# Spreading every norm's inverse root over the partitions: matrix products against transposes

## The chip, the cores and the metric

The kernel runs on one core of one Trainium2 chip. The metric is device time in microseconds (us) of one execution, taken as the median of several runs. Times inside an execution come from one profiled execution, and are counted from the start of its span.

## The reference

One layer of an encoder over 1024 tokens of width 1024, in float32: a norm, one combined projection, two kinds of attention side by side (group A: a sliding window with a sink; group B: a neighbourhood on a 16 x 64 grid), a norm for each group, one output projection, then a norm, a gated MLP with a convolution of width 3 along the tokens, and a last norm. Every norm is the same function:

```python
def rmsnorm(x, g):
    xf = x.astype(jnp.float32)
    y = xf * lax.rsqrt(jnp.mean(xf * xf, axis=-1, keepdims=True) + EPS)
    return (y * g.astype(jnp.float32)).astype(x.dtype)
...
hn = rmsnorm(h, norm_mix[l])
proj = jnp.einsum('bsd,de->bse', hn, w_in[l])
...
mix = jnp.concatenate([rmsnorm(o_a, norm_a[l]), rmsnorm(o_b, norm_b[l])], axis=-1)
h = h + jnp.einsum('bse,ed->bsd', mix, w_out[l])
hn = rmsnorm(h, norm_ffn[l])
h = h + conv_gated_mlp(hn, w_gate[l], w_up[l], conv_w[l], conv_b[l], w_down[l])
return rmsnorm(h, norm_final)
```

So five norms are computed: the first, those of group A and of group B, the middle one ahead of the MLP, and the last.

## The kernel before, in words

**Layout.** Activations are kept transposed: a tile has 128 features on its partitions and the 1024 tokens along its free axis, worked on in two halves h of 512 tokens. Large products split each float32 operand into a high and a low part of a reduced type and issue three products of 128x512 for each pair of blocks (lines 144 to 146 in `block`, 866 to 868 in `group`).

**The norms.** The sum over features runs across partitions, so TensorE does it. ACT squares the tiles and DVE adds them; then `inverse_narrow` multiplies each block of 128 tokens of the squares by a column of ones (L181), which leaves the sums in a narrow tile: token t of block c sits on partition t, column c. ACT takes the root (L184) and DVE the reciprocal (L185) of this 128 x 4 tile `v`. The features' tiles need the value of a token on all partitions, along the free axis. This is the work of `widen` (L192): for each of its n columns, a 128x128 block of the PSUM tile `wide` gets v's column along its free axis, the same on all partitions. The weights operand is v's column repeated 128 times (`to_broadcast`), the streamed operand is the identity `ident`, a slice of the tile `cst`.

**Who calls widen.** Four columns are one half of 512 tokens.
- First norm: both halves in one go; ACT copies them into `rstd1` (L626), with which DVE evacuates the first projections (`evacuate`, L199).
- Group A: `wide_a`, both halves between attention units; ACT copies them into `rstda` (L708), with which DVE scales `mixa` (L711).
- Group B: one half, then weights and some filling products, then the other half; DVE scales `mixb` straight from PSUM (L834), ACT makes the high part (L835), DVE the low part `mgl` (L836). Around it DVE also adds group A's output products to the residual (L553), and makes the low parts of output weights (L821).
- Middle norm: the first half between output products of the second half, the second half between the first products of the MLP; DVE scales the tiles in `normed` (L895).
- Last norm: `finish` calls widen twice, once for DVE (L1287) and once for a copy by ACT (L1281) that POOL uses for two of the eight feature tiles (L1285). It is called with four columns for the second half, and with two columns for each quarter of the first half; the last call stands at the end of the kernel, with the output's DMAs behind it (L1288).

**Transposes elsewhere.** The kernel already issues transposes of float32 tiles of 128x128 on TensorE: `split_v` turns the values (tile `vt`, L280, eight of them per call), and the attention units turn the probabilities (tile `pt`, L389 in group A and L462 in group B).

**What sets the order.** TensorE's order is the program's own: its queue is under a manual schedule, and group A's and B's attention, the projections and the output products are interleaved by hand (a generator `filler`, taken from at set rates). The order of DVE and ACT is chosen by a scheduler while the program is built, from estimated durations and priorities; a change in what an instruction is thought to cost can change that order. In the MLP's start, four units of weights come in at once (`pure`, `head_weights`): loads into three buffers `raw` (SP's queue), sums and differences of weights on DVE (L904, L912), and their high and low parts on ACT and DVE (L855, L856). `Gated` evacuates the products z and y with DVE (L1016, L1022, L1026).

PSUM tiles named by tag share two banks per tag; `widen` draws from the tag `pt` in every call, as the transposed probabilities do.

Of the kernel before, what the change touches and what calls it, by code (L numbers as in the profile page):

```python
# [53 lines left out]
def hybrid_layer(tc, xT, w_in, w_out, w_gate, w_up, w_down, small, sink, rpb, consts, rope, out):  # L54
    nc = tc.nc
    with ExitStack() as ctx:
# [19 lines left out]
        def bank(name, tag):  # L76
            return psum.tile([128, HALF], F32, name=name, tag=tag)
# [12 lines left out]
        ident = cst[:, K_ID:K_ID + 128]  # L90
# [85 lines left out]
        def inverse_narrow(sqs, dim, tag, n=4):  # L176

            ps = bank("ss", tag)
            for i, sq in enumerate(sqs):
                for c in range(n):  # L180
                    nc.tensor.matmul(ps[:, c:c + 1], sq[:, c * 128:(c + 1) * 128], ones[:, 0:1], start=c == 0 and i == 0,  # L181
                                     stop=i == len(sqs) - 1, skip_group_check=True)
            v = cpool.tile([128, 4], F32, name="v4", tag="v4", bufs=4)
            nc.scalar.activation(v[:, 0:n], ps[:, 0:n], AF.Sqrt, bias=eps, scale=float(D) / dim)  # L184
            nc.vector.reciprocal(v[:, 0:n], v[:, 0:n])  # L185
            return v

        def widen(v, tag, n=4):

            wide = bank("sw", tag)  # L190
            for c in range(n):
                nc.tensor.matmul(wide[:, c * 128:(c + 1) * 128], v[:, c:c + 1].to_broadcast([128, 128]), ident,  # L192
                                 start=c == 0, stop=True, skip_group_check=True)
            return wide


# [428 lines left out]
        for h in range(2):  # L625
            nc.scalar.activation(rstd1[:, tsl(h)], widen(vs1[h], "pt"), AF.Copy)  # L626
# [77 lines left out]
        def wide_a():  # L704
            live["op"] += 1
            norm["a"] = big("rstda", "op")
            for h in range(2):
                nc.scalar.activation(norm["a"][:, tsl(h)], widen(norm["v"][h], "pt"), AF.Copy)  # L708
# [120 lines left out]
        for h in range(2):  # L829
            wide = widen(vb2[h], "pt")  # L830
            for i in range(4):
                x = mix[4 + i][:, tsl(h)]
                hi, lo = (t[:, tsl(h)] for t in mg[4 + i])
                nc.vector.scalar_tensor_tensor(x, x, col(C_NB + i), wide, op0=ALU.mult, op1=ALU.mult)  # L834
                nc.scalar.activation(hi, x, AF.Copy)  # L835
                nc.vector.tensor_tensor(lo, x, f32(hi), op=ALU.subtract)  # L836
            if h == 0:
                wo = [load_wo(d, wpool) for d in range(2)]
                fill(3)
# [86 lines left out]
        for h in range(2):  # L926
            for d in range(KT):
# [6 lines left out]
                if h == 1 and d == 1:  # L934
                    v = inverse_narrow([total[0]], D, "pt")
# [5 lines left out]
                if h == 1 and d == 2:  # L941
                    wide = widen(v, "pt")
# [137 lines left out]
        v = inverse_narrow([total[1]], D, "pt")  # L1080
        units[1].p2()
        wide = widen(v, "pt")
# [375 lines left out]
```

## Time and profile before

| what | us |
|---|---|
| median of 3 runs | 1103.57 (1101.68 to 1103.87) |
| the profiled execution | 1103.74 |
| its span, first to last instruction | 1101.9 |
| DVE busy | 858.5 (78%) |
| ACT busy | 552.9 (50%) |

The profile lists each instruction with its start, length, engine, line and tiles (out<-in). "PE" is TensorE's products and "PEld" its weight loads, which overlap the products; "xN" counts instructions. In brackets stands how long the engine had been idle before an instruction and what released it. The list of waits sums these idle times by the waiting instruction. The length of a product includes time in which the next is already running, so that the distance from one start to the next is the measure of what a product costs in a stream. In the view by windows, each row gives a window, its length, and the busy time and number of instructions of TensorE, its loads, DVE, ACT and POOL, then the granted clock of TensorE (1.00 is full), the busy share of the DMA engines and GB/s.

### The profile page before, as it was taken

To read this page: it belongs to the slowest core of one execution; us is meant where nothing else is said; L and a number is where in the kernel's file an instruction comes from. 1 tells how busy PE (TensorE), PEld (TensorE's weight loads), DVE (VectorE), ACT (ScalarE), POOL (GpSimd) and SP (SyncE) were. 2 spreads that over 40 slices of the span, in tenths; PEclk is the share of its full clock that TensorE was granted. 3 is DMA by queue.
4 is the path that set the end of the run, shared out by engine and by line. 5 is a ranking of instruction groups with operands and counts; after the bars stand their busy time and mean duration, and the time that the engine had idled before them with its cause. 6 is when DMAs were issued, how large, how long until landed. Compare 5 with 4: busy or idle time off the path is not lost.

```text
span 1101.9 us, 15051 instructions
## 1 busy us (share of the span) xinstructions
PE 1079.2 (98%) x5190; PEld 901.0 (82%) x5190; DVE 858.5 (78%) x1565; ACT 552.9 (50%) x1042; POOL 109.2 (10%) x188
## 2 busy tenths in 40 slices
PE   8999999999999999999999999999999999999996
PEld 6888788888888888887788888888888778888886
DVE  7688787667688689899988877887787857886843
ACT  7457676556676544545434343433434643533631
POOL 2223333222232100000000000000000000000001
PEclk9999999999999999999999999999999999999998
DMA  7222122222225136214342232322233888774824
GB/s 271 72 72 68 48 58 68 77 76 77 77 67 159 68 127 240 96 39 162 124 161 89 104 124 77 132 98 106 96 112 109 277 288 289 258 227 165 270 79 154
DMA packets 68365, 144.95 MB, mean 132 GB/s; under 512 B 8128, under 2 KB 18880, under 8 KB 68288
## 3 DMA queue, kind: packets, MB, share of 16 engines
q1 hardware_dynamic: 57632, 118.16, 33.6%
q10 hardware_dynamic: 10656, 25.82, 6.2%
q8 instruction: 41, 0.67, 0.2%
q14 instruction: 36, 0.29, 0.1%
HBM read 103.58 MB, written 28.57 MB: 120 GB/s over the span
## 4 chain that ended last, share of the span: by engine, by line
PE 86%; DVE 7%; DMA 3%; ACT 2%; issue 2%; POOL 0%; SPq 0%; DVEq 0%; ACTq 0%; POOLq 0%
PE pj L144 7%; PE pj L145 7%; PE pj L146 7%; PE dn L866 6%; PE dn L867 6%; PE dn L868 6%; PE z L868 5%; PE z L866 5%; PE z L867 5%; PE x L866 3%; PE s L327 3%; PE x L867 3%; PE x L868 3%; PE y L868 3%; PE y L867 3%; PE y L866 3%
## 5 line engine op out<-in xcount | busy, mean ns | idle before, releaser
L866 PE MATMUL dn<-xd,whi 128*128 128x512 f32 (+1 forms) x330 | 124.9, 378 | 2.3 <-ACT c L1294 2.3
L868 PE MATMUL dn<-xd,wlo 128*128 128x512 f32 (+1 forms) x330 | 124.4, 377 | 0.0
L867 PE MATMUL dn<-xd,whi 128*128 128x512 f32 (+1 forms) x330 | 124.2, 377 | 0.0
L855 ACT ACTIVATE whi<-ws 128x512 fp32r<-128x512 f32 (+1 forms) x100 | 60.2, 624 | 122.3 <-DVE ws L972 80.4
L866 PE MATMUL z<-hg,whi 128*128 128x512 f32 x264 | 103.0, 390 | 1.0 <-DVE gs L1022 1.0
L144 PE MATMUL pj<-xgh,whi 128*128 128x512 f32 x248 | 104.0, 419 | 0.0
L868 PE MATMUL z<-hg,wlo 128*128 128x512 f32 x264 | 103.1, 390 | 0.6 <-DVE wlo L856 0.6
L867 PE MATMUL z<-hg,whi 128*128 128x512 f32 x264 | 102.7, 389 | 0.0
L353 ACT ACTIVATE p<-p,nm 128x385 f32<-128x385 f32 (+3 forms) x128 | 75.3, 588 | 51.7 <-DVE nm L349 50.6
L146 PE MATMUL pj<-xgh,wlo 128*128 128x512 f32 x248 | 97.6, 393 | 0.0
L145 PE MATMUL pj<-xgl,whi 128*128 128x512 f32 x248 | 97.2, 392 | 0.0
L357 POOL TENSOR_SCALAR p<-p,sm 128x384 f32<-128x384 f32 (+1 forms) x128 | 74.1, 591 | 215.9 <-DVE sm L355 201.5
L856 DVE TENSOR_TENSOR wlo<-raw,whi 128x512 fp32r<-128x512 f32 (+1 forms) x102 | 66.6, 673 | 22.7 <-ACT whi L855 22.4
L363 DVE TENSOR_TENSOR pl<-pt,ph 128x384 fp32r<-128x384 f32 (+2 forms) x108 | 63.0, 588 | 24.5 <-ACT ph L362 23.2
L855 ACT ACTIVATE whi<-raw 128x512 fp32r<-128x512 f32 (+1 forms) x102 | 60.5, 613 | 42.7 <-DMA raw<-in_w_down_dram 19.3
L856 DVE TENSOR_TENSOR wlo<-ws,whi 128x512 fp32r<-128x512 f32 (+1 forms) x100 | 66.8, 683 | 18.7 <-ACT whi L855 18.7
L1285 POOL TENSOR_TENSOR h<-h,wide 128x256 f32<-128x256 f32 (+1 forms) x6 | 5.4, 920 | 718.7 <-ACT wide L1281 718.7
L1177 ACT ACTIVATE xd<-xd 128x512 fp32r<-128x512 f32 x77 | 47.1, 627 | 55.0 <-DMA xd<-x 53.5
L866 PEld LDWEIGHTS dn<-xd,whi 128*128 128x128 f32 x330 | 62.5, 189 | 14.0 <-ACT c L1294 2.8
L868 PEld LDWEIGHTS dn<-xd,wlo 128*128 128x128 f32 x330 | 62.4, 189 | 11.5
L867 PEld LDWEIGHTS dn<-xd,whi 128*128 128x128 f32 x330 | 62.5, 190 | 11.1
L362 ACT ACTIVATE ph<-pt 128x384 fp32r<-128x384 f32 (+2 forms) x108 | 55.2, 515 | 32.0 <-PE pt L462 25.0
(211 smaller groups left out, 2686.0 us busy)
## 6 DMA issues: line engine op xcount, KB each, us to landing
xd<-x SPq DMA_DIRECT2D x77, 256.0 KB, 5.1
raw<-in_w_down_dram SPq DMA_DIRECT2D x72, 256.0 KB, 3.4
raw<-in_w_gate_dram SPq DMA_DIRECT2D x22, 512.0 KB, 3.6
raw<-in_w_up_dram SPq DMA_DIRECT2D x22, 512.0 KB, 3.8
x<-c ACTq DMA_DIRECT2D x22, 512.0 KB, 2.6
raw<-in_w_in_dram SPq DMA_DIRECT2D x32, 256.0 KB, 3.0
raw<-in_w_down_dram SPq DMA_DIRECT2D x36, 192.0 KB, 3.9
x<-t ACTq DMA_DIRECT2D x11, 512.0 KB, 2.6
```

Source lines behind the costliest of these rows:

```text
L144: nc.tensor.matmul(ps, w[0], x[0][:, tsl(h)], start=first, stop=False)
L145: nc.tensor.matmul(ps, w[0], x[1][:, tsl(h)], start=False, stop=False)
L146: nc.tensor.matmul(ps, w[1], x[0][:, tsl(h)], start=False, stop=last)
L353: nc.scalar.activation(p[:, j, 0:e], p[:, j, 0:e], AF.Exp, bias=nm, scale=-1.0, accum_out=sm[:, j:j + 1])
L357: nc.gpsimd.tensor_scalar(p[:, i, 0:m], p[:, i, 0:m], sm[:, i:i + 1], 1.0, op0=ALU.mult, op1=ALU.mult)
L362: nc.scalar.activation(ph[:, 0:n], ps[:, 0:n], AF.Copy)
L363: nc.vector.tensor_tensor(pl[:, 0:n], ps[:, 0:n], f32(ph[:, 0:n]), op=ALU.subtract)
L855: nc.scalar.activation(hi, src, AF.Copy)
L856: nc.vector.tensor_tensor(lo, src, f32(hi[:, :, :]), op=ALU.subtract)
L866: nc.tensor.matmul(ps, w[0], x[0], start=first and i == 0, stop=False, skip_group_check=True)
L867: nc.tensor.matmul(ps, w[0], x[1], start=False, stop=False, skip_group_check=True)
L868: nc.tensor.matmul(ps, w[1], x[0], start=False, stop=last and i == len(ws) - 1, skip_group_check=True)
```

## The change

In `widen`, the product of the repeated column and the identity is written as a transpose of the repeated column, with the same operands, into the same place. Flags of accumulation that the product carried go with it.

```diff
             wide = bank("sw", tag)
             for c in range(n):
-                nc.tensor.matmul(wide[:, c * 128:(c + 1) * 128], v[:, c:c + 1].to_broadcast([128, 128]), ident,
-                                 start=c == 0, stop=True, skip_group_check=True)
+                nc.tensor.transpose(wide[:, c * 128:(c + 1) * 128], v[:, c:c + 1].to_broadcast([128, 128]), ident)
             return wide
```

Nothing else is edited. In the built program, the order of instructions on TensorE, POOL and SP is as before. The scheduler gives DVE another order in four places (the evacuation L199 behind the first norm; L834, L836 and L553 around group B's norm; L885, L890, L904 and L856 around the first half of the middle norm; L904, L1016 and L1022 in the MLP's start) and ACT in two (L184 and L855 around the first half of the middle norm; L855, L873 and L1011 in the MLP's start). Everything in the steady part of the MLP and after it keeps its order.

## The prediction

> **What bounds the kernel now.** I read the page first, then the waits of TensorE, then the spread's own line beside that of an operation that already is a transpose, then the order of time around each place where the spread runs.
>
> ```profile
> span 1101.9 us, 15051 instructions
> ...
> PE 1079.2 (98%) x5190; PEld 901.0 (82%) x5190; DVE 858.5 (78%) x1565; ACT 552.9 (50%) x1042; POOL 109.2 (10%) x188
> ```
>
> TensorE works for 98% of the span, so what it is spared shortens the run unless a wait behind it takes the gain. These are the waits of TensorE, in us, number and longest:
>
> ```profile
> PE dn L866 <- ACT c L1294: 2.3, 1, 2.3
> ...
> PE sw L192 <- DVE v L185: 0.6, 1, 0.6
> ...
> PE sw L192 <- DVE pl L363: 0.3, 1, 0.3
> ```
>
> The largest is 2.3 us and there are few; the spread (sw) itself waits twice. So I treat TensorE's own stream as the bound nearly everywhere and look for the exceptions one by one.
>
> **The change: what one spread costs.** The line of the spread (L192), and the transposes of split_v (L280), whose operands have the same shape, type and places (data loaded as weights, identity streamed):
>
> ```profile
> L192 PEld LDWEIGHTS sw<-cst,v x96: 185/190/192, 39.4 to 1094.3; 128*128 128x128 f32 x96
> L192 PE MATMUL sw<-cst,v x96: 270/275/376, 39.6 to 1094.4; 128*128 128x128 f32 x96
> ```
>
> ```profile
> L280 PEld LDWEIGHTS vt<-cst,t x48: 138/141/146, 44.6 to 301.7; 128*128 128x128 f32 x48
> L280 PE MATMUL vt<-cst,t x48: 270/273/332, 44.8 to 301.8; 128*128 128x128 f32 x48
> ```
>
> widen is called 14 times: twice each for the first norm, group A, group B and the middle norm, and six times in the last one. Ten of the calls spread four columns, the last four spread two: 48 columns. The trace has 96 records, so a float32 matrix product leaves **two** records, each with its weight load. split_v runs 6 times with 8 transposes each, 48, and the trace has 48 records: a float32 transpose leaves **one**. The change therefore takes 48 pairs of load and product out of TensorE's stream.
>
> What a record is worth is read from start to start, not from its 275 ns, since they overlap. Eight records of the spread:
>
> ```profile
> 390.49 1.05 PE L192 MATMUL sw<-cst,v 128*128 128x128 f32 x8
> 391.29 0.48 PE L144 MATMUL pj<-mgh,whi 128*128 128x512 f32 x1
> ```
>
> that is 0.80 us. Sixteen of them, in the last norm:
>
> ```profile
> 1071.82 1.95 PE L192 MATMUL sw<-cst,v 128*128 128x128 f32 x16
> 1073.52 0.36 PE L866 MATMUL dn<-xd,whi 128*128 128x256 f32 x1
> ```
>
> 1.70 us. Eight transposes, and four:
>
> ```profile
> 44.81 1.03 PE L280 MATMUL vt<-cst,t 128*128 128x128 f32 x8
> 45.60 0.48 PE L144 MATMUL pj<-xgh,whi 128*128 128x512 f32 x1
> ```
>
> ```profile
> 151.65 0.60 PE L389 MATMUL pt<-cst,p 128*128 128x128 f32 x4
> 152.00 0.48 PE L144 MATMUL pj<-xgh,whi 128*128 128x512 f32 x1
> ```
>
> 0.79 and 0.35 us. Each further record costs (1.70 - 0.80) / 8 = 0.11 us, and a transpose costs no more; the change halves their number. A call of four columns saves 0.80 - 0.35 = **0.45 us**; two calls back to back save 1.70 - 0.79 = **0.91 us**. That the weights are one column repeated, and not a full tile, is new for a transpose but not for the load: the spread of before loads the same repeated column. This unknown lies between the transposes' own rows and a record of twice the length, which would eat the whole gain; I take the transposes' rows, as the nearest.
>
> **Place by place.** *First norm, pair:* 0.91. Behind it stand ACT's copy and then DVE:
>
> ```profile
> 41.30 0.69 DVE L199 TENSOR_TENSOR t<-pj,rstd 128x512 f32<-128x512 f32 x1 [3.20 <-ACT rstd L626]
> ```
>
> DVE idles 3.20 us for the spread's result, so the consumers start earlier with it and TensorE's later waits on them move along. In the changed program DVE takes both halves of one projection, then both of the other, instead of alternating; the first rotation can then start after two products instead of three. I count nothing for that.
>
> *Group A, two separate calls:*
>
> ```profile
> 289.97 1.06 PE L192 MATMUL sw<-cst,v 128*128 128x128 f32 x8
> 291.36 1.16 PE L192 MATMUL sw<-cst,v 128*128 128x128 f32 x8 [0.34 <-DVE pl L363]
> 292.28 0.47 PE L144 MATMUL pj<-xgh,whi 128*128 128x512 f32 x1
> ```
>
> ```profile
> 290.75 0.56 DVE L363 TENSOR_TENSOR pl<-pt,ph 128x384 fp32r<-128x384 f32 x1 [0.25 <-ACT ph L362]
> ```
>
> The second call waits for its PSUM bank, which DVE frees at 290.75 + 0.56 = 291.31 whatever the first call costs. So the first call's gain turns into 0.45 us more of that wait: **0**. The second saves 0.45, and what ACT and DVE do with its result moves with it.
>
> *Group B, two calls:* both inside a stream of products with no wait near: 2 x 0.45 = 0.90. Here the changed program orders DVE's L834, L836 and L553 otherwise: both L553 come sooner, and one operation that stood ahead of the second now stands behind it, ahead of the weights for the next products (L821).
>
> ```profile
> 402.06 0.69 DVE L553 TENSOR_TENSOR h<-pj,xr 128x512 f32<-128x512 f32 x1 [0.17 <-PE pj L146]
> ...
> 405.39 0.68 DVE L821 TENSOR_TENSOR wo<-raw,wo 128x512 fp32r<-128x512 f32 x1
> ```
>
> DVE waits for TensorE at that L553 already (0.17 us), so the weights come up to one operation, 0.68 us, later. No wait of TensorE for L821 is in its list, so there is room of unknown size: between 0 and 0.68 us I charge 0, and keep the other end for rival 1.
>
> *Middle norm, first half:* 0.45, same stream. *Second half:*
>
> ```profile
> 459.09 1.05 PE L192 MATMUL sw<-cst,v 128*128 128x128 f32 x8
> 459.90 0.48 PE L866 MATMUL x<-hg,whi 128*128 128x512 f32 x1
> ```
>
> ```profile
> 459.73 0.69 DVE L856 TENSOR_TENSOR wlo<-ws,whi 128x512 fp32r<-128x512 f32 x1 [2.29 <-ACT whi L855]
> 460.34 2.72 DVE L895 SCALAR_TENSOR_TENSOR h<-h,par,sw 128x512 f32<-128x512 f32 x4
> ...
> 492.86 0.69 DVE L1022 TENSOR_TENSOR gs<-z,c 128x512 f32<-128x512 f32 x1 [0.22 <-PE z L868]
> ```
>
> ```profile
> 460.00:513.00 53.00, 52.77 (x233) 43.06 (x232) 52.53 (x83) 26.28 (x42) 0.00 (x0) 1.00 0.17 56
> ```
>
> ```profile
> 512.83 0.50 PE L868 MATMUL z<-hg,wlo 128*128 128x512 f32 x1 [0.23 <-DVE wlo L856]
> ```
>
> From 460 to 513 DVE is busy 52.53 of 53 us (third busy figure of the window). It starts on L895 only after L856, not at the spread's end, so a faster spread does not start it sooner. TensorE comes 0.45 us earlier to a DVE that can give back only its small waits, such as the 0.22 us at 492.86, and TensorE's own wait at 512.83 grows by the rest. Between 0 and 0.45 I take 0.30.
>
> *Last norm:* the pair 0.91, then two calls of two columns back to back, eight records, 0.45. The last two calls stand in the tail, on the chain that ended last:
>
> ```profile
> 1093.58 0.70 PE sw L192 x4
> 1094.28 0.02 issue
> 1094.30 0.48 DVE h L1287
> ```
>
> DVE begins after the first call, four records. Two fewer save 2 x 0.11 = 0.22; the second call feeds ACT and POOL, which end before DVE does.
>
> **Sum:** 0.91 + 0.45 + 0.90 + 0.45 + 0.30 + 0.91 + 0.45 + 0.22 = 4.59 us. The profiled execution took 1103.74 us: 1103.74 - 4.6 = **1099.1 us**. It lay 0.17 us above the median of the three runs, less than the 2.2 us between their ends, so I leave it there.
>
> **The rivals.** (1) *A DVE-bound stretch takes more.* The gains ahead of the last norm, 3.0 us, all come before waits on DVE; only the last norm's 0.91 + 0.45 + 0.22 = 1.58 has none behind it. If half of the 3.0 us goes, 3.1 are left: 1100.7; if all goes, 1102.2. For it: the 52.53 of 53 us. Against: before 460, DVE idles for the spread or for TensorE. 0.24.
>
> (2) *The transposes do not overlap* and so the kernel gets slower. At 273 ns each, start to start, 48 take 13.1 us; 96 records at 1.70 / 16 take 10.2: 2.9 us more, 1106.6. It decides from 0.21 us per transpose. Against it stand 0.79 us for eight. A clock that fell would do the same; in the window that holds those eight it was full (the 1.00):
>
> ```profile
> 44.00:46.00 2.00, 2.00 (x15) 1.75 (x14) 1.38 (x4) 0.39 (x1) 0.00 (x0) 1.00 0.28 66
> ```
>
> [...] 0.04.
>
> (3) *Nothing is halved*: a transpose of a repeated column leaves two records. Then the time is that of before, 1103.7. 48 records for 48 calls of L280 speak against it. 0.03.
>
> (4) *DVE's new order costs.* Ahead of the L856 at 459.73 now stands the fourth difference of weights (L904), one place later than before, behind a load from DRAM. DVE's 2.29 us idle at 459.73 covers its 0.69 us and 1.6 us of lateness of that load; beyond, each us goes through the busy stretch to TensorE. Two us late past that cover would give 1101 to 1102; slower than before it makes the kernel only past 4.6. 0.07, of which 0.03 slower.
>
> **How the numbers follow.** The forecast, gains from 4.0 to 5.3, has 0.62. The low end is all 48 records (48 x 0.11 = 5.3, 1098.4) less half of the 2.2 us between the runs: 1097.2. The high end goes to 1101.6, most of rival 1; beyond lie its tail, and rivals 2, 3 and part of 4. A measurement of this kernel can tell about 0.2%, 2.2 us, from no change. Faster: 0.62 and three quarters of 0.24, 0.80; same: the rest of it, rival 3 and the milder part of 4, 0.13; slower: 0.07.
>
> **What would show it.** Right: 48 records of L192, 5142 on TensorE in all; spacing of eight (now four) from 0.80 to about 0.35, of the pairs from 1.70 to 0.79; the wait before group A's second call up from 0.34 to about 0.8; the wait at 512.83 up by up to 0.45. Wrong: two records per transpose, a spacing over 0.2 us, a granted clock under 1.00 at these places, or waits on DVE between 41 and 513 that grow by more than 1 us in all.

## The result, and the profile after

The kernel after takes 1096.26 us, median of 8 runs (1092.64 to 1098.07), where the kernel before took 1101.22 in 8 runs beside them (1100.26 to 1103.87): ratio 0.9938, 95% interval 0.9922 to 0.9954. The forecast was 1099.1, range 1097.2 to 1101.6: the sign is right, the gain larger than forecast, and the time lies below the range. Over the whole study, 78 runs of the kernel before have a mean of 1102.14 (standard error 0.20; 1098.42 to 1106.91) and 20 of the kernel after 1095.35 (0.43). The gain is **6.8 us, with a standard error of 0.5**, and 4.6 was forecast. ("Give or take" stands for a standard error everywhere below.)

The page of the kernel after; its profiled execution took 1097.33 us.

```profile
span 1095.5 us, 14955 instructions
...
PE 1073.6 (98%) x5142; PEld 895.3 (82%) x5142; DVE 857.4 (78%) x1565; ACT 550.6 (50%) x1042; POOL 109.0 (10%) x188
```

TensorE has 5142 records where it had 5190: 48 are gone, and the other engines' counts are as before. The spread's line (lines past 192 stand one lower now):

```profile
L192 PEld LDWEIGHTS sw<-cst,v x48: 132/136/137, 39.5 to 1089.3; 128*128 128x128 f32 x48
L192 PE MATMUL sw<-cst,v x48: 270/273/322, 39.8 to 1089.4; 128*128 128x128 f32 x48
```

One record per transpose, and its load is shorter too (136 against 190 ns). In the order of time, the middle norm's second half and the last norm's pair:

```profile
455.93 0.60 PE L192 MATMUL sw<-cst,v 128*128 128x128 f32 x4
456.28 0.48 PE L865 MATMUL x<-hg,whi 128*128 128x512 f32 x1
```

```profile
1068.71 1.03 PE L192 MATMUL sw<-cst,v 128*128 128x128 f32 x8
1069.50 0.36 PE L865 MATMUL dn<-xd,whi 128*128 128x256 f32 x1
```

Four transposes take 0.35 us from start to the next product, eight 0.79, as the prediction took from the other transposes. A repeated column costs here what a full tile costs, 0.79 us for eight.

Subtracting the starts of one and the same product in two traces gives the **shift** of TensorE's stream, and its step across a place is what that place gained. For the second half of the middle norm: the spread began at 459.09 and begins at 455.93, 3.16 earlier; the product behind it began at 459.90 and begins at 456.28, 3.62 earlier. The place gained 0.46. In this manner:

| place | forecast | measured |
|---|---|---|
| first norm, pair | 0.91 | 0.91 |
| group A, two calls | 0 + 0.45 | 0.60 |
| group B, two calls | 0.90 | 0.46 + 0.46 |
| middle norm, first half | 0.45 | 0.46 |
| middle norm, second half | 0.30 | 0.46 |
| last norm, pair and quarter | 0.91 + 0.45 | 0.92 + 0.46 |
| tail | 0.22 | 0.28 |
| sum | 4.59 | 5.01 |

So the places of the spread account for 5.0 us, and some **1.8 us** of the 6.8 were gained where no spread stands. Whether they come back, and from where they are, is what the experiments had to find.

The two places where the forecast had taken something off, group A's second call and TensorE's wait in the MLP's start, in the kernel after; between them ACT's copy of group A's first spread in the kernel before:

```profile
289.19 0.60 PE L192 MATMUL sw<-cst,v 128*128 128x128 f32 x4
289.84 0.59 ACT L707 ACTIVATE rstda<-sw 128x512 f32<-128x512 f32 x1
289.98 0.56 DVE L362 TENSOR_TENSOR pl<-pt,ph 128x384 fp32r<-128x384 f32 x1 [0.24 <-ACT ph L361]
290.49 0.65 PE L192 MATMUL sw<-cst,v 128*128 128x128 f32 x4 [0.69 <-ACT rstda L707]
```

```profile
291.06 0.60 ACT L708 ACTIVATE rstda<-sw 128x512 f32<-128x512 f32 x1 [0.34 <-PE sw L192]
```

```profile
509.21 0.50 PE L867 MATMUL z<-hg,wlo 128*128 128x512 f32 x1 [0.24 <-DVE wlo L855]
```

The wait before the second call did grow, from 0.34 to 0.69 us, but by 0.35 and not by the first call's 0.45. The profile now names ACT's copy of the first spread as what released it; that copy ends at 290.43. DVE's L362 ends only at 290.54, 0.05 us later than the call's start, so it is not what the call waited for. In the kernel before it was the other way: the call started 0.05 us behind DVE's end, and ACT's copy ended only at 291.66, 0.30 us behind that start. All three profiles of each kernel agree in this. At 509.21 the wait is 0.24 where it was 0.23: nothing was given back.

### The profile page after: what moved, and what is told of

It is laid out like the page before. It is cut to its first block, busy times and chain, and to the rows that moved or that the text cites. A ratio compares the mean times of both kernels' runs of the same rounds, so it can differ in the third digit from the quotient of the medians.

```text
span 1095.5 us, 14955 instructions
## 1 busy us (share of the span) xinstructions
PE 1073.6 (98%) x5142; PEld 895.3 (82%) x5142; DVE 857.4 (78%) x1565; ACT 550.6 (50%) x1042; POOL 109.0 (10%) x188
## 4 chain that ended last, share of the span: by engine, by line
PE 85%; DVE 9%; DMA 2%; ACT 2%; issue 1%; POOL 0%; SPq 0%; DVEq 0%; ACTq 0%; POOLq 0%
PE pj L144 7%; PE pj L145 7%; PE pj L146 7%; PE dn L865 6%; PE dn L867 6%; PE dn L866 6%; PE z L867 4%; PE z L865 4%; PE z L866 4%; PE s L326 3%; PE x L865 3%; PE x L866 3%; PE x L867 3%; PE y L867 3%; PE y L865 3%; PE y L866 3%
## 5 line engine op out<-in xcount | busy, mean ns | idle before, releaser
L855 DVE TENSOR_TENSOR wlo<-raw,whi 128x512 fp32r<-128x512 f32 (+1 forms) x102 | 66.5, 672 | 22.2 <-ACT whi L854 21.9
L362 DVE TENSOR_TENSOR pl<-pt,ph 128x384 fp32r<-128x384 f32 (+2 forms) x108 | 63.0, 588 | 24.5 <-ACT ph L361 23.3
L855 DVE TENSOR_TENSOR wlo<-ws,whi 128x512 fp32r<-128x512 f32 (+1 forms) x100 | 66.8, 683 | 18.4 <-ACT whi L854 17.3
```

Source lines behind the costliest of these rows:

```text
L362: nc.vector.tensor_tensor(pl[:, 0:n], ps[:, 0:n], f32(ph[:, 0:n]), op=ALU.subtract)
L855: nc.vector.tensor_tensor(lo, src, f32(hi[:, :, :]), op=ALU.subtract)
```

## The experiments

The kernels differ from before or after in `widen` alone or in one call of it. For kernels in which some calls are transposes and some products, `widen` has one more argument:

```diff
-        def widen(v, tag, n=4):
+        def widen(v, tag, n=4, turned=True):
             wide = bank("sw", tag)
             for c in range(n):
-                nc.tensor.transpose(wide[:, c * 128:(c + 1) * 128], v[:, c:c + 1].to_broadcast([128, 128]), ident)
+                if turned:
+                    nc.tensor.transpose(wide[:, c * 128:(c + 1) * 128], v[:, c:c + 1].to_broadcast([128, 128]), ident)
+                    continue
+                nc.tensor.matmul(wide[:, c * 128:(c + 1) * 128], v[:, c:c + 1].to_broadcast([128, 128]), ident,
+                                 start=c == 0, stop=True, skip_group_check=True)
```

Lines below stand three higher in them. "Ratio" is always to runs of the kernel before in the same series.

### Both kernels again

No edit.

> The kernel before, unchanged, once more. In the two profiled executions the changed kernel's span is 6.4 us shorter, of which 4.5 lie ahead of the last spread, 0.3 in it, and 1.6 behind the end of DVE's last products, where only the output's transfers land (1096.74 to 1101.9 before, 1091.97 to 1095.5 after). Theory A (the records alone count, the landing varies by itself from run to run): time within 0.2% of the kernel before, and the stretch from DVE's end to the end of the span may be anywhere from 3.5 to 5.2 us. Theory B (the change shortens the landing too): again 5.0 to 5.3 us there.

> The changed kernel, unchanged, once more. Theory A: 4.4 to 5.2 us faster than the kernel before in the median of many runs (0.40 to 0.47%), with a landing stretch anywhere from 3.5 to 5.2 us. Theory B: 6 to 7 us faster (0.55 to 0.65%), landing stretch 3.4 to 3.7 us each time.

> The changed kernel, unchanged, for more runs beside the next three. Over all runs so far it takes 6.6 us less than the kernel before (14 and 43 runs), while the shifts of TensorE's stream at the spreads and the tail's own 0.28 add up to 5.1. Theory A (records alone; what is over 5.1 is the scatter of the runs): 4.6 to 5.6 us faster than the kernel before (0.42 to 0.51%). Theory C (a product costs more than its two records, somewhere that the sites do not show): 6.0 to 7.0 us (0.55 to 0.63%).

Measured: the kernel before 1102.32 us (12 runs), ratio 1.0003 (0.9987 to 1.0018). The kernel after 1095.97, ratio 0.9937 (0.9917 to 0.9957), and 1094.8, ratio 0.9932 (0.9916 to 0.9949), 6 runs each. The gain repeats three times at 0.62 to 0.68%. All three profiles of after have the same steps at the spreads, to 0.01 us. The size of the gain is the one that theories B and C had, but B's reason does not hold: the stretch from DVE's end to the end of the span took 4.20 us in the repeated before, where B has 5.0 to 5.3. Theory C is put to the test by `twice` below.

### Part of the calls

`last_only` has transposes in `finish` alone (16 of 48 columns), `all_but_last` everywhere else (32).

```diff
-            wide, again = widen(v, "pt", n), widen(v, "pt", n)
+            wide, again = widen(v, "pt", n, True), widen(v, "pt", n, True)
```

(False in `all_but_last`; in `last_only` the default of `turned` is False.) The scheduler gives `last_only` the order of before on every engine, and `all_but_last` that of after.

> The kernel before with transposes only in the last norm (the calls from finish, 16 of the 48 columns); the order of all engines is that of the kernel before. Theory A: 0.93 + 0.46 + 0.28 = 1.7 us faster (0.15%), 5174 records on TensorE. Theory B: 3.3 us faster (0.30%), since the landing is shortened by the last spreads.

> The changed kernel with matrix products again in the last norm (32 of the 48 columns are transposes); DVE and ACT have the order of the changed kernel. Theory A: 3.0 to 3.3 us faster than the kernel before (0.28%): the shift of the stream by the last norm, 3.1 us in the changed kernel's trace. Theory B: the same 3.0 to 3.3 us. A rival for the earlier stages, that part of the shift there (0.4 us near 352 us) is one run's accident and not the change: 2.7 us. If it is above 4 us, the gain does not come record by record.

Measured: `last_only` 1100.05 us, ratio 0.998 (0.9968 to 0.9992); `all_but_last` 1096.74, ratio 0.9954 (0.9937 to 0.9971). Against the mean of all runs of before, their means (1100.09 and 1096.82) lie 2.1 and 5.3 us lower, which add up to more than the whole gain, within their scatter (0.5 and 0.7). In the trace `last_only` gains 0.92 + 0.46 at its two places inside the stream and nothing at the other spreads; with the tail's 0.22 to 0.28 that is 1.6 to 1.7. So it has about what its spreads are worth (theory A's 1.7, not B's 3.3). `all_but_last` gained more than both theories had, and more than the 4 us named beforehand as the sign that the gain does not come record by record alone: the surplus sits with the other 32 columns: their places sum to 5.01 - 1.66 = 3.35, and 5.3 was measured.

### More records of the same kind

`twice` issues each transpose twice into the same place, `four_times` four times.

```diff
-                nc.tensor.transpose(wide[:, c * 128:(c + 1) * 128], v[:, c:c + 1].to_broadcast([128, 128]), ident)
+                for _ in range(2):
+                    nc.tensor.transpose(wide[:, c * 128:(c + 1) * 128], v[:, c:c + 1].to_broadcast([128, 128]), ident)
```

> Every transpose is issued twice into the same place, so the spread leaves 96 records again, all transposes; DVE and ACT have nearly the order of the kernel before. Theory A: the time of the kernel before, within 0.1%. Theory C: still 1.0 to 1.9 us faster than the kernel before (0.09 to 0.17%). If transposes did not overlap, it would be slower than the kernel before by over 2 us.

> Every transpose is issued four times: 192 records, 144 more than in the changed kernel. Theory A: 144 x 0.11 = 15.8 us more than the changed kernel, less up to 0.7 that a wait in group A takes up, so 10 to 11 us slower than the kernel before (0.9 to 1.0%). A price of 0.14 us per record, as 6.6 us over 48 would have it: 20 us more than the changed kernel, 13.5 slower than before (1.2%).

Measured: `twice` 1102.1 us, ratio 0.9996 (0.998 to 1.0011); `four_times` 1114.64, ratio 1.0102 (1.0085 to 1.012). With 96 records, as many as before, the time is that of before, though each is a transpose and each load a short one. So the number of records is what counts, and theory C, by which `twice` would still be 1.0 to 1.9 us faster than before, is not borne out (its mean is 0.1 us slower, give or take 0.7). `four_times` has 144 more than after and a mean of 1114.02 (0.60), 18.7 us above after's, 0.13 per record; 15.8 was expected by the records alone, and 20 by a price of 0.14. Its pair in the last norm:

```profile
1080.21 3.66 PE L193 MATMUL sw<-cst,v 128*128 128x128 f32 x32
1083.62 0.36 PE L866 MATMUL dn<-xd,whi 128*128 128x256 f32 x1
```

3.41 us for 32, 0.107 each. In its trace all spreads together take 14.3 us more than in after's, the wait in group A being taken up; the other 4.4 us are not at the spreads and were not followed up. The clock was full in the window of these 32:

```profile
1080.21:1083.62 3.41, 3.41 (x33) 3.40 (x32) 2.15 (x4) 0.00 (x0) 0.00 (x0) 1.00 0.00 0
```

That ends rival 2: over these 3.41 us, a run of transposes neither loses its overlap (0.107 us from start to start) nor lowers the clock (1.00). A longer run was not tried. What sets the pace was not tried either; the loads' own median length in this trace is 137 ns.

### One spread less in the last norm

`once_last` is the kernel after, with ACT's copy reading the spread that DVE reads.

```diff
-            wide, again = widen(v, "pt", n), widen(v, "pt", n)
+            wide = widen(v, "pt", n)
...
-            nc.scalar.activation(copy[:, cols], again[:, 0:128 * n], AF.Copy)
+            nc.scalar.activation(copy[:, cols], wide[:, 0:128 * n], AF.Copy)
```

> The changed kernel, but finish spreads the last norm's root once instead of twice: ACT's copy for POOL reads the same PSUM tile as DVE. 8 transposes fewer, 40 records of the spread. By records: 0.44 us less in the pair and 0.22 less before the last quarter, nothing in the tail, where DVE already starts after the first call: 0.66 us faster than the changed kernel (0.06%). Rival: ACT and DVE reading one bank delay each other, and the tail gets 0.2 to 0.4 us longer than that of the changed kernel.

Measured: 1093.91 us, ratio 0.993 (0.9909 to 0.9951). In the trace the pair gains 0.44 and the quarter 0.22 more than in after, as expected, but the tail, put at nothing, gives 0.57 back:

```profile
1084.29 0.56 PE L192 MATMUL sw<-cst,v 128*128 128x128 f32 x2 [0.64 <-DVE v L185]
1084.88 0.38 ACT L1280 ACTIVATE wide<-sw 128x256 f32<-128x256 f32 x1 [0.93 <-PE sw L192]
1085.30 2.44 DVE L1286 SCALAR_TENSOR_TENSOR h<-h,par,sw 128x256 f32<-128x256 f32 x6 [1.16 <-ACT wide L1280]
```

DVE starts 1.01 us after the spread, behind ACT's copy of the same tile, where it took 0.44 in after. The net is 0.1 us, which these runs cannot tell from after (means 1095.03, give or take 1.07, and 1095.35). The rival had the tail's loss right in kind and too small in size. The second spread earns its place in the tail, not inside the stream.

### Where the rest comes from: DVE's order

Outside the spreads, the shift of TensorE's stream moves in several stretches. By 30 us it differs from that of before's first profile by -0.3 to 2.5 us, and between 850 and 910 us it changes by -4.1 to 0.6; both kernels scatter there, and three profiles of each cannot show a difference between them. Two stretches remain in which kernels differ and not only profiles: 345 to 357 and 434 to 458 us (times of before). In the second, the kernels with the old order of DVE lost up to 1 us in some profiles, and those with the new order never. The old order puts the first difference of weights (L904), which waits for a load from DRAM, *ahead* of a sum of squares (L890), an addition to the residual (L885) and the scaling of the middle norm's first half (L895); the new order puts it behind them. Group B's two calls alone turn this order, so they can be parted from the rest: `b_only` has transposes in group B alone (8 columns) and the new order there, `all_but_b` everywhere else (40) and the old one. A third profile of before goes with them.

```diff
-            wide = widen(vb2[h], "pt")
+            wide = widen(vb2[h], "pt", turned=False)
```

(True in `b_only`, with False as the default.)

> Only group B's norm is spread with transposes (two of the 14 calls, 8 of the 48 columns); the other twelve calls keep their products. That alone moves the first difference of up weights (L904 in the kernel before) behind the first half's middle spread in DVE's order, as the kernel after has it; the evacuation behind the first norm and the MLP's start keep their places. Theory of sites alone: group B's two calls give 0.46 each, 0.92, so about 0.9 us below the kernel before's mean of 1102.25, 1101.3 (ratio 0.9992). Theory that DVE's order around the first half of the middle norm is worth something as well: the stretch 434 to 458 shows no shift, as in the kernels that have every transpose, where the kernels with the old order showed 0, 0, 0.88, 0.98 and 1.03; that adds 0.5 on average, so 1100.8 (ratio 0.9987). The two lie within the scatter of the medians, so the stretch in the trace decides: 0 by the order theory, 0 to 1 by the other.

> Group B's two calls keep their products, the other twelve calls are transposes (40 of 48 columns). DVE then keeps the kernel before's order around group B's norm and around the middle norm, with the first difference of up weights ahead of the first half's middle spread, while all other spreads are short. Theory of sites alone: 5.05 less 0.92 is 4.1, so 1102.25 less 4.1, 1098.1 (ratio 0.9963), and what lay beyond the sites in the kernel after (1.8 us) is to be missing only if it hangs on the order. If it doesn't hang on the order, but on TensorE being earlier by then, the time is 1102.25 less 6.0, 1096.3 (ratio 0.9946). In the trace, by the order theory the stretch 434 to 458 loses up to 1 us to a wait of DVE for the weights' load, in some profiles and not in others (two of the five profiles with the old order lost nothing), so that only a loss there speaks for the theory, and no loss leaves it open.

> The kernel before once more, for a third profile of it. By the theory that the differences beyond the sites hang on DVE's order: 434 to 458 shifts by 0 to 1 us against the first profile, 345 to 357 by -0.35 to +0.45, and the stretch from the end of DVE's last products to the span's end takes 3.8 to 5.2. By the theory that these differences are the run's own scatter: 345 to 357 and the last stretch fall where the kernel after's profiles lie (-0.35 and 3.5 to 3.8).

Measured: `b_only` 1101.05 us, ratio 0.9999 (0.9984 to 1.0014); `all_but_b` 1097.74, ratio 0.9961 (0.9947 to 0.9974); the profiled run of before 1101.45. The times alone don't decide: `all_but_b`, at a mean of 1097.2 (0.74), lies between the 1098.1 and 1096.3 expected, and `b_only` (mean 1101.67, 0.71) is as near to before as to its own 1100.8 and 1101.3. The traces do. `all_but_b`, DVE and then TensorE:

```profile
428.81 0.17 DVE L185 RECIPROCAL v<-v 128x4 f32<-128x4 f32 x1
...
431.74 0.69 DVE L907 TENSOR_TENSOR ws<-ws,raw 128x512 f32<-128x512 f32 x1 [2.09 <-DMA raw<-in_w_gate_dram]
432.35 0.69 DVE L893 TENSOR_TENSOR s<-s,s 128x512 f32<-128x512 f32 x1
432.95 0.68 DVE L888 TENSOR_TENSOR h<-pj,h 128x512 f32<-128x512 f32 x1
433.55 2.06 DVE L898 SCALAR_TENSOR_TENSOR h<-h,par,sw 128x512 f32<-128x512 f32 x3
```

```profile
447.98 0.50 PE L869 MATMUL x<-hg,whi 128*128 128x512 f32 x1 [0.20 <-DVE h L888]
```

DVE stands 2.09 us before the load, and the norm's scaling (L898) and everything behind it come late. TensorE loses 0.92 us in this stretch, although 40 of its 48 columns are short. `b_only` and after:

```profile
432.61 0.69 DVE L888 TENSOR_TENSOR h<-pj,h 128x512 f32<-128x512 f32 x1
433.50 2.06 DVE L898 SCALAR_TENSOR_TENSOR h<-h,par,sw 128x512 f32<-128x512 f32 x3 [0.20 <-PE sw L195]
```

```profile
430.23 0.69 DVE L884 TENSOR_TENSOR h<-pj,h 128x512 f32<-128x512 f32 x1 [0.17 <-PE pj L146]
430.83 2.06 DVE L894 SCALAR_TENSOR_TENSOR h<-h,par,sw 128x512 f32<-128x512 f32 x3
...
445.70 0.69 DVE L903 TENSOR_TENSOR ws<-ws,raw 128x512 f32<-128x512 f32 x1
```

In these two no load stands ahead of the scaling; the first difference comes at 445.70 and finds its data there. The stretch loses 0. The third profile of before loses 0.96, with a longer wait where the first had 0.87 us. The first and the third profile:

```profile
432.43 0.69 DVE L904 TENSOR_TENSOR ws<-ws,raw 128x512 f32<-128x512 f32 x1 [0.87 <-DMA raw<-in_w_gate_dram]
```

```profile
434.40 0.69 DVE L904 TENSOR_TENSOR ws<-ws,raw 128x512 f32<-128x512 f32 x1 [2.09 <-DMA raw<-in_w_gate_dram]
...
450.63 0.50 PE L866 MATMUL x<-hg,whi 128*128 128x512 f32 x1 [0.21 <-DVE h L885]
```

Shifts against the first profile of before, over the kernels with at most two records per column (positive is a loss):

| stretch | old order: before, again_before, third_before, twice, last_only, all_but_b | new order: after, again_after, third_after, once_last, all_but_last, b_only |
|---|---|---|
| 420 to 432.5 | 0.01 at most in all six | 0, 0, 0.74, 0, 0, 0.52 |
| 434 to 458 | 0, 0, 0.96, 0.90, 1.03, 0.92 | 0 in all six |

The second row has the old order losing in four of six profiles, whatever the form of the spreads. It follows the wait for the load: a wait of 0.87 us at the first difference cost TensorE nothing, and those of 1.88 to 2.20 us cost 0.90 to 1.03. `four_times`, which has the old order there too, waited 2.31 us and lost 0.99. So the path from the load to TensorE is shown. The first row takes part of it back: in two profiles with the new order, a load of up weights is late ahead of the sums (L912). Whether that hangs on the order or is chance, these runs leave open. The means of both rows together are 0.64 and 0.21, so the order is worth about **0.4 us** on average, from six profiles a side, give or take 0.24. The three profiles of before and the three of after by themselves differ by less than 0.1 here (means 0.32 and 0.25), so how much of the measured gain this is stays open.

### The copy in group B

The other stretch, 345 to 357, waits for a copy of a key tile, and the chain that ended last runs over it in before:

```profile
342.19 3.27 DMA q<-kb
345.52 6.34 DMA kb<-ka
```

TensorE's load for the scores stands behind it, and the loads of the residual and of output weights share the queue:

```profile
351.90 0.19 PEld L327 LDWEIGHTS s<-kb,q 128*128 128x128 f32 x1 [0.40 <-DMA kb<-ka]
```

Among the DMA issues of 343 to 352 us, the copy issued just ahead of it took this long from issue to landing, in before and in after:

```profile
ka<-kb SPq DMA_DIRECT2D x1, 256.0 KB, 6.0
```

```profile
ka<-kb SPq DMA_DIRECT2D x1, 256.0 KB, 4.0
```

The six profiles in which group A's and the first norm's spreads have half the records (after three times, `all_but_last`, `once_last`, `all_but_b`) have no wait here and shift by -0.36 each. Of the six in which these have as many records as before, five wait and one does not: 0, -0.36, 0.06, 0.43, 0.38 and -0.07, mean 0.07. That is **0.4 us** with the change, give or take 0.1. What is shown is that it goes with the early spreads and not with group B's, nor with DVE's order around group B and the middle norm (`b_only` against `all_but_b`). DVE's other order behind the first norm (L199) comes and goes with the same six profiles, so these runs do not part it from the spreads. That the residual's load, issued 1.45 us earlier while both copies are issued at nearly the same times as before, is out of the copies' way sooner is only argued; it was not tried.

## Why the prediction was right in its sign and wrong in its size

**What held.** One record per transpose, 0.11 us for each record saved, 0.45 and 0.91 per call and pair, at every place but group A. The experiments with more records confirm the price at 0.107 us. Rivals 2 and 3 are refuted, by the spacing of 32 and by 48 records. Rival 1, that a busy DVE takes the gain, did not come: in after's first profile no gain was taken back behind the spreads. The covered lateness that rival 4 named stayed covered:

```profile
454.77 0.69 DVE L903 TENSOR_TENSOR ws<-ws,raw 128x512 f32<-128x512 f32 x1 [0.50 <-DMA raw<-in_w_gate_dram]
```

**The steps that failed.** The largest is the level from which the gain was taken off (point 5); the others made the gain itself too small.

1. *"The second call waits for its PSUM bank, which DVE frees at 290.75 + 0.56 = 291.31 whatever the first call costs."* It was put at 0 and brought 0.10 us; the second call brought 0.51, not 0.45. In before, the reading of the release fits: DVE's end at 291.31, the call at 291.36, and ACT's copy still running. But it was carried over to the changed program, where the call starts ahead of DVE's end and is named as released by ACT's copy, which moves with the first call. Why the call waits for another reader there, these runs do not show.
2. *"Between 0 and 0.45 I take 0.30"* for the middle norm's second half: all of it was kept. As forecast, DVE does not start on the scaling sooner (457.17 against 460.34, the 3.17 us from ahead of the spread). But it *can* give back its small waits, and these were just enough: by the L856 ahead of TensorE's wait it is 3.62 us earlier. Its waits of 0.08, 0.16 and 0.22 us, at 472.39, 479.26 and 492.86, are gone, and one of 0.15 us is new. Of the 53 us it was idle for 0.47, which is the number to hold against 0.45; the 52.53 alone looks like a bound. That the one just covers the other is luck. The last row is before, the one ahead of it after:

```profile
509.06 0.69 DVE L855 TENSOR_TENSOR wlo<-raw,whi 128x512 fp32r<-128x512 f32 x1
```

```profile
512.68 0.70 DVE L856 TENSOR_TENSOR wlo<-raw,whi 128x512 fp32r<-128x512 f32 x1
```

3. *Rival 4, "DVE's new order costs."* On average over the profiles the sign was the other way, by 0.4 us, give or take 0.24. The step looked at the one difference that stands later in the new order and at its cover, and not at the first difference, which in the old order stood in front of the norm's scaling behind a load. The row that shows it, 0.87 us at 432.43, was in the trace of before, but in that profile it cost TensorE nothing, and the prediction does not name it.
4. *The sum counted only the places of the spread*, and put nothing on what an earlier stream does to transfers between them. The copy of group B belonged there: it is on the chain of before, with 6.34 us, and the stretch that waits for it gained 0.4 us.
5. *"It lay 0.17 us above the median of the three runs, less than the 2.2 us between their ends, so I leave it there."* The profiled 1103.74 lies 1.6 us above the mean of 78 runs, 1102.14. That alone moves the forecast from 1099.1 to 1097.5. In the result's own eight runs the median of before is lower still, 1101.22, and 4.6 less than that is 1096.6, against 1096.26 measured. That these two medians differ by 4.96, so near to the forecast gain, is luck of eight runs: their means differ by 5.9, and all runs by 6.8. The range's low end took half of the scatter of three runs with the full 5.3, and had no room for a gain beyond the records.

**The account.** From the forecast to the mean of 20 runs is 1099.1 - 1095.35 = 3.8 us: 1.6 from the level of before, and 6.8 - 4.6 = 2.2 from the gain. Of the latter, 0.4 is at the spreads (points 1 and 2, and 0.06 in the tail). The traces point to 0.4 for the copy in group B and 0.4 for DVE's order. Together that makes 5.0 + 0.4 + 0.4 = 5.8, against 6.8 give or take 0.5, so for 1.0 us no place was found.

Two candidates can be looked at. The landing at the end, from the end of DVE's last products to the span's end, is 5.20, 4.20 and 3.80 us in the three profiles of before and 3.57 in each of those of after. But it is 3.77 in `last_only` and 3.79 in `all_but_last`, with the last spreads short in one and long in the other, and 3.77 to 3.80 in `twice`, `b_only` and `all_but_b` as well, so it is not shown to hang on the change. The clock is not the reason: the granted clock, listed for 70 of the runs of before and for the 20 of after, has a mean of 0.9965 in the one and 0.9964 in the other; at full load that difference is 0.1 us.

**What stays open:** the 1.0 us, two standard errors of the gain; the sizes of the terms for the copy and for DVE's order, which rest on six profiles a side; the cause of the copy's earlier landing, which is argued; and what sets the landing at the end, which was not tested.

## What to carry to other kernels

When operands allow both, write a float32 spread or turn on TensorE as a transpose (here that spared one record of 0.11 us per column): count the records in the trace first, and price each by the distance between starts, not by its length. When the program's order is chosen by a scheduler, read the new order for what now stands *behind* a load from DRAM and also for what no longer does: in `all_but_b` DVE's wait of 2.09 us for such a load held up the norm's scaling behind it, and in the runs in which this wait was 1.88 to 2.31 us, 0.90 to 1.03 us of it reached TensorE; of the 0.87 us in the first profile of before nothing did. And where a gain is 0.5%, take the level from many runs: one execution's distance from the mean was a quarter of the effect.

## What the runs showed of the hardware that was not expected

**Behind a wait of 2.33 us the clock was at half in one run, and behind 2.42 us at full in another.** Near 904 us TensorE waits for ACT's copy of a product out of PSUM (L1294), for 0.32 to 3.45 us in ten of the thirteen profiles. The window 904 to 909 of before, of its repetition, and of the third profile of it; the column of the clock is the third from the right:

```profile
904.00:909.00 5.00, 4.45 (x13) 3.50 (x14) 4.96 (x9) 4.70 (x10) 0.00 (x0) 0.66 0.84 270
```

```profile
904.00:909.00 5.00, 5.00 (x24) 4.14 (x23) 4.87 (x9) 3.46 (x8) 0.00 (x0) 1.00 0.89 279
```

```profile
904.00:909.00 5.00, 3.73 (x16) 3.08 (x17) 3.61 (x7) 3.71 (x8) 0.00 (x0) 1.00 0.89 266
```

The first waited 2.33 us and then ran at half rate from 905.12 to 908.53, with 0.43 us from one start to the next where it is 0.23 afterwards; over the eight products of this stretch that costs 1.6 us:

```profile
904.55 0.50 PE L866 MATMUL dn<-xd,whi 128*128 128x512 f32 x1 [2.33 <-ACT c L1294]
...
905.55 0.63 PE L866 MATMUL dn<-xd,whi 128*128 128x512 f32 x1
905.98 0.63 PE L867 MATMUL dn<-xd,whi 128*128 128x512 f32 x1
...
908.53 0.39 PE L867 MATMUL dn<-xd,whi 128*128 128x512 f32 x1
908.76 0.39 PE L868 MATMUL dn<-xd,wlo 128*128 128x512 f32 x1
```

The third profile waited 2.42 us there and kept the full clock:

```profile
905.27 0.50 PE L866 MATMUL dn<-xd,whi 128*128 128x512 f32 x1 [2.42 <-ACT c L1294]
```

What parts the two, these runs do not show.

Both kinds occur with both forms of the spread (the kernel after has a clock of 0.84 from 904 to 909, and its repetition 1.00 from 904 to 912), so this is scatter of single runs and no part of the gain; it is one reason why a single execution can lie 1.6 us off.
